# Feed-forward gate and up by seven block products instead of eight, down projection in six parts

## The chip, the cores and the metric

One core of a Trainium2 chip runs the kernel. The metric is the device time of one execution in microseconds (us), the median of the runs shown. The engines that matter here are PE (TensorE, matmuls), DVE (VectorE), ACT (ScalarE), POOL (GpSimd) and SP (SyncE, which issues the DMAs); each runs its own list of instructions in order, and semaphores make one wait for another.

## The reference

Two layers of a backbone over 512 latent tokens, with a context of 256 tokens that only the first layer updates. Each layer mixes tokens, projects back and then does a feed-forward step (`D_MODEL` 1024, `FFN_HIDDEN` 2816), all in float32:

```python
def swiglu(h, w_gate, w_up, w_down):
    return (jax.nn.silu(h @ w_gate) * (h @ w_up)) @ w_down
...
    for l in range(DEPTH):
        need_ctx = l < DEPTH - 1
        mx = (sc @ w_ada[l] + b_ada[l]).reshape(-1, N_MOD, 1, D_MODEL)
...
        h = modulate(rms_norm(x, g_ffn[l]), mx[:, 3], mx[:, 4])
        x = x + mx[:, 5] * swiglu(h, w_gate[l], w_up[l], w_down[l])
        if need_ctx:
            hc = modulate(rms_norm(ctx, g_ffn[l]), mc[:, 3], mc[:, 4])
            ctx = ctx + mc[:, 5] * swiglu(hc, w_gate[l], w_up[l], w_down[l])
```

## The kernel before

Tokens lie along the free axis, features on the 128 partitions: `xT` holds 8 blocks k of 128 features. Layer l=0 works on 768 tokens (512 latent and 256 context, `sts`), layer l=1 on the 512 latent ones. A float32 product is made of three fast products: each operand is split into a rounded high part and the rest (`h`, `l`), and high·high, low·high and high·low are summed in PSUM. So each 128x128 block of weights meets a stretch of tokens in three matmuls (`gemm`, L104).

A weight tile (`wtiles`, L205 to L217) is a DMA of 128x1024 into `wr`, a cast on ACT for the high part `wh` (L216), and a subtraction on POOL for the low part `wl` (L217). `wr`, `wh` and `wl` have two buffers each; `kh`, `kl` are the same for tiles that are kept.

The feed-forward step is the end of `layer()` (from L1302). The hidden 2816 features are 22 tiles t. For each t two weight tiles (gate, then up) are multiplied with all 8 blocks of `fh`, `fl` into two PSUM tiles `acc_gu` of two banks each (tag `b2`, four buffers), in stretches of 512 tokens and, in layer 0, 256 more. Then ACT takes the silu of the gate (L1340), DVE multiplies it by the up product (L1343, `av`), ACT rounds it (L1346, `ah`) and DVE subtracts (L1347, `al`). `FFN_PARTS` cuts the 22 tiles into three parts; at the end of a part the down projection multiplies the part's 7 or 8 tiles with 8 column blocks m of `w_dn` into `acc_d`, and DVE adds the result, scaled by `mod`, to `xT` (L1361). In the last part the column blocks in `KEPT` keep their weights and are done one stretch of tokens after the other.

```python
b2 = lambda nm: ps.tile([P, 1024], F32, tag="b2", name=nm, bufs=4)
...
for (t0, t1) in FFN_PARTS:
    for t in range(t0, t1):
        for j in range(2):
            gemm(acc, *w, hh, hl, sts if t else segs[1:])
            next(ada, None)
    for m in range(KD):
        gemm(acc, wh, wl, ah, al, sts)
        for st_ in sts:
            add(m, st_, acc[:, st_])
        next(ada, None)
```

`ada_rows` (L254) is a side task of layer 0's feed-forward step: 56 loads `wada` of 512 KB, each followed by two long DVE multiplications with a sum (`junk`), which give the modulation of what comes later. One step of it is taken at each `next(ada)`. Its first part, `mod[0][:, 5]`, scales the down projection of layer 0.

The norm ahead of the step (`norm_mod`, L297 to L305) makes `fh` and `fl` block by block from `xT`; it runs in two stretches of tokens, and the first two products start while it runs. The order of the instructions on each engine is set when the kernel is built, by a scheduler that takes the program's dependences, tile by tile; two products in one PSUM tile share its buffer, which is free again only when the last reader of either is done.

## Time and profile before

| what | value |
|---|---|
| median of 3 runs | 2154.72 us (2153.34 to 2160.51) |
| profiled execution | 2156.67 us, its span 2154.9 us |
| PE busy | 2003.9 us (93% of the span) |
| DVE, ACT, POOL busy | 1244.0, 707.8, 839.9 us |
| mean granted PE clock | 0.962 |
| layer 0's feed-forward step | about 684 to 1220 us of the span |
| layer 1's feed-forward step | about 1780 us to the end |

The span is the profiled time from the first to the last instruction; 1.8 us of the execution lie around it. A busy share says how much of the time an engine had an instruction in it. The granted clock is TensorE's: 1.00 is 2.4 GHz, 0.50 is 1.2 GHz.

### The profile page before, as it was taken

The page shows a single profiled execution, that of the slowest core. Times are in us where ns is not written, and L with a number is a line of the kernel's source. Part 1 is how long each engine was busy: PE and PEld are TensorE (multiplying, and loading weights), DVE is VectorE, ACT ScalarE, POOL GpSimd, SP SyncE. Part 2 cuts the span into 40 slices and gives each one's busy share as a digit, 9 for nine tenths or more (in the row PEclk, how much of TensorE's full clock was granted, in tenths as well). Part 3 has the DMA queues.
Part 4 walks back from the last instruction along what each step waited for, and adds up shares of the span by engine and source line. Part 5 has one row for each costly group of instructions (what it writes and reads, how often), then busy time and mean ns, then how long its engine had stood idle before and what let it go on. Part 6 is the DMA issues. An engine that isn't in the chain of part 4 may idle for free. (4 is left out here: it accounts for less than half of the span.)

```text
span 2154.9 us, 32133 instructions
## 1 busy us (share of the span) xinstructions
PE 2003.9 (93%) x12770; PEld 1694.8 (79%) x12770; DVE 1244.0 (58%) x2107; ACT 707.8 (33%) x1381; POOL 839.9 (39%) x602
## 2 busy tenths in 40 slices
...
GB/s 275 81 81 156 65 142 82 149 147 129 103 50 98 100 125 157 91 135 129 135 127 75 119 93 59 104 123 73 143 65 88 82 92 67 97 98 94 102 96 91
DMA packets 119278, 232.57 MB, mean 108 GB/s; under 512 B 30484, under 2 KB 55956, under 8 KB 119000
## 3 DMA queue, kind: packets, MB, share of 16 engines
...
## 5 line engine op out<-in xcount | busy, mean ns | idle before, releaser
L217 POOL TENSOR_TENSOR wl<-wr,wh 128x1024 fp32r<-128x1024 f32 (+2 forms) x188 | 440.0, 2341 | 716.4 <-ACT wh L216 708.0
L216 ACT CAST wh<-wr 128x1024 fp32r<-128x1024 f32 (+2 forms) x190 | 193.5, 1019 | 730.2 <-PE acc_gu L104 289.3
L104 PE MATMUL acc_gu<-fh,wh 128*128 128x512 f32 (+1 forms) x1024 | 359.2, 353 | 6.1 <-ACT fh L304 5.3
L104 PE MATMUL acc_gu<-fl,wh 128*128 128x512 f32 (+1 forms) x1024 | 361.0, 353 | 3.6 <-DVE fl L305 3.6
L104 PE MATMUL acc_gu<-fh,wl 128*128 128x512 f32 (+1 forms) x1024 | 360.2, 352 | 0.0
L104 PE MATMUL acc_in<-hh,wl 128*128 128x512 f32 (+1 forms) x640 | 227.3, 359 | 23.2 <-POOL wl L217 23.2
L104 PE MATMUL acc_in<-hh,wh 128*128 128x512 f32 (+1 forms) x640 | 229.9, 363 | 17.9 <-ACT xp L491 7.4
L104 PE MATMUL acc_in<-hl,wh 128*128 128x512 f32 (+1 forms) x640 | 229.8, 360 | 3.2 <-DVE hl L305 2.0
L1343 DVE TENSOR_TENSOR av<-acc_gu,av 128x768 f32<-128x768 f32 (+1 forms) x44 | 36.3, 825 | 337.5 <-PE acc_gu L104 330.0
L104 PEld LDWEIGHTS acc_gu<-fh,wh 128*128 128x128 f32 x1024 | 194.1, 190 | 33.2 <-ACT fh L304 6.9
L104 PEld LDWEIGHTS acc_gu<-fl,wh 128*128 128x128 f32 x1024 | 195.1, 191 | 29.8 <-DVE fl L305 3.9
L104 PEld LDWEIGHTS acc_gu<-fh,wl 128*128 128x128 f32 x1024 | 195.0, 190 | 26.5
L104 PEld LDWEIGHTS acc_in<-hh,wh 128*128 128x128 f32 x640 | 125.7, 197 | 43.4 <-ACT xp L491 9.1
L104 PEld LDWEIGHTS acc_in<-hh,wl 128*128 128x128 f32 x640 | 125.6, 198 | 43.0 <-POOL wl L217 25.4
L104 PE MATMUL acc_d<-al,wh 128*128 128x512 f32 (+1 forms) x444 | 157.2, 354 | 0.0
L104 PE MATMUL acc_d<-ah,wh 128*128 128x512 f32 (+1 forms) x444 | 157.2, 354 | 0.0
L104 PE MATMUL acc_d<-ah,wl 128*128 128x512 f32 (+1 forms) x444 | 156.1, 354 | 0.0
L254 DVE CUSTOM_DVE_ANT_0 junk<-wada,scb 128x1024 f32<-128x1024 f32 x112 | 145.6, 1300 | 6.3 <-DMA wada<-w_adaT 3.2
L104 PEld LDWEIGHTS acc_in<-hl,wh 128*128 128x128 f32 x640 | 126.5, 198 | 25.9 <-DVE hl L305 4.6
L501 DVE SCALAR_TENSOR_TENSOR cy<-xp,cw,cy 128x770 f32<-128x770 f32 (+1 forms) x96 | 128.2, 1335 | 22.2 <-ACT cy L499 18.4
L1361 DVE SCALAR_TENSOR_TENSOR xT<-acc_d,mod,xT 128x512 f32<-128x512 f32 (+1 forms) x76 | 46.5, 635 | 155.1 <-PE acc_d L104 155.1
L1347 DVE TENSOR_TENSOR al<-av,ah 128x768 fp32r<-128x768 f32 (+1 forms) x44 | 100.4, 2281 | 35.2 <-ACT ah L1346 35.2
...
## 6 DMA issues: line engine op xcount, KB each, us to landing
wr<-w_gu SPq DMA_DIRECT2D x88, 512.0 KB, 3.5
wada<-w_adaT SPq DMA_DIRECT2D x56, 512.0 KB, 3.4
wr<-w_in SPq DMA_DIRECT2D x48, 512.0 KB, 3.5
...
wada<-w_ada SPq DMA_DIRECT2D x24, 512.0 KB, 3.4
...
wr<-w_dn SPq DMA_DIRECT2D x16, 512.0 KB, 3.6
...
```

The lines of the kernel that those rows point to most:

```text
L104: nc.tensor.matmul(out, lhsT, rhs, start=start, stop=stop)
L216: S.copy(out=hi[:, sl], in_=raw[:, sl])
L217: eng.tensor_tensor(out=lo[:, sl], in0=raw[:, sl], in1=hi[:, sl].bitcast(F32), op=ALU.subtract)
L254: V.tensor_tensor_reduce(out=junk, in0=w, in1=scb[:, s], scale=1.0, scalar=0.0, op0=ALU.mult, op1=ALU.add, accum_out=mod[l][:, part, j, s: ...
L501: stt(out=y[:, :wid], in0=xp[:, j:j + wid], scalar=w_(j), in1=y[:, :wid], op0=ALU.mult, op1=ALU.add)
L1343: tt(out=av[:, :nT], in0=accs[1][:, :nT], in1=av[:, :nT], op=ALU.mult)
L1347: after.append(tt(out=l_[:, :nT], in0=av[:, :nT], in1=h_[:, :nT].bitcast(F32), op=ALU.subtract))
L1361: stt(out=xT[:, m, st_], in0=acc, scalar=mod[l][:, 5, m, s:s + 1], in1=xT[:, m, st_], op0=ALU.mult, op1=ALU.add)
```

## The change

For tiles t from 2 on, the two weight tiles of t and the activations are each cut into 2x2 blocks: the weights into gate and up (rows) by two halves of k, the activations into two halves of k by two halves of the tokens (`nh` = 384 in layer 0, 256 in layer 1). The eight block products become seven of sums of blocks (`seven`). Four activation sums t1 to t4 are made once per layer, four weight sums s1 to s4 for every t (`weights`), and seven additions from PSUM put the results together. Tiles 0 and 1 keep eight products (`first`), now done in two halves of the tokens. `split2` makes high and low parts; `FFN_ENG` says which engine does each weight sum and each low part (V is DVE, G is POOL). The down projection is done in six parts instead of three, with four buffers of `ah` and `al` instead of eight, and all 8 column blocks of the last part are kept. `ada_rows` has one `wada` buffer instead of two, and makes one column instead of two for four of layer 1's six parts. Lines of the changed kernel are numbered anew: `gemm` is L109, the weight sums L1402, the splits L1334 (ACT) and L1335, the additions from PSUM L1424, `junk` L264, the product of silu and up L1459, `ah` L1462, `al` L1463, the addition to `xT` L1479.

```diff
-FFN_PARTS = ((0, 8), (8, 15), (15, 22))
-
-KEPT = (4, 5, 6, 7)
+FFN_PARTS = ((0, 4), (4, 8), (8, 12), (12, 15), (15, 18), (18, 22))
+FFN_BUFS = 4
+
+FFN_ENG = (("VVVV", "GVGV"), ("VVVV", "GVVV"))
+
+ADA_T_ = (0, 3, 3, 3) + (0, 1) * 9
+
+KEPT = (0, 1, 2, 3, 4, 5, 6, 7)
...
+            ns = 2 if l == 0 or part < 2 else 1
-                w = sb.tile([P, D], F32, tag="wa", name="wada", bufs=2)
+                w = sb.tile([P, D], F32, tag="wa", name="wada", bufs=1)
                 nc.sync.dma_start(out=w, in_=a["w_adaT"][l, part, j])
                 with tc.issue_after(after[-1].ins):
-                    for s in range(2):
+                    for s in range(ns):
                         junk = sb.tile([P, D], F32, tag="junk", name="junk", bufs=1)
...
+        def split2(dst, src, eng):
+            S.copy(out=dst[0], in_=src)
+            eng.tensor_tensor(out=dst[1], in0=src, in1=dst[0].bitcast(F32), op=ALU.subtract)
+
+        def ffn_norm(k, cols, rs):
+            c, t = int(cols == CTX), xf[k][:, cols]
+            stt(out=t, in0=xT[:, k, cols], scalar=e.gs[l][:, 1, k, c:c + 1], in1=rs[:, :cols.stop - cols.start], op0=ALU.mult, op1=ALU.mult)
+            S.activation(out=t, in_=t, func=AF.Identity, bias=mod[l][:, 3, k, c:c + 1])
+            if k >= 4:
+                to = [(b2x[k - 4], cols, 0)]
+            else:
+                to = [(ts[k], slice(max(cols.start, h.start), min(cols.stop, h.stop)), h.start) for ts, h in ((b11, H[0]), (b12, H[1]))]
+            for hl_, c_, c0 in to:
+                if c_.start < c_.stop:
+                    split2([x[:, c_.start - c0:c_.stop - c0] for x in hl_], xf[k][:, c_], G if k % 2 else V)
+
...
+        fslot = lambda n: [fw.tile([P, 1024], F32R, tag="f" + x, name="f" + x, bufs=2)[:, 0:n] for x in "hl"]
+        wslot = lambda n: [e.wp.tile([P, 1024], F32R, tag="w" + x, name="w" + x, bufs=2)[:, 0:n] for x in "hl"]
...
+        at = lambda acc, h: acc[:, 512 * h:512 * h + nh]
+        blocks = (b11 + b21, b12 + b22)
+        first = [(whole(i // 2, i % 2, wslot if i < 2 else fslot), b2("acc_gu")) for i in range(3)]
+        for h, cols in enumerate(segs):
+            if h:
                 rs = e.rstd_of(xT, b2, sb, (cols,))[0]
             for k in range(KD):
-                e.norm_mod(xT, l, 1, sb, hh, hl, k, cols, rs)
-        second = [wtiles(a["w_gu"][l, 1, j], 1024, sg, 2) for j in range(2)]
+                ffn_norm(k, cols, rs)
+            for k in range(KD):
+                ws = slice(k * P, (k + 1) * P)
+                for w, acc in first:
+                    mm3(nc, at(acc, h), (w[0][:, ws], w[1][:, ws]), blocks[h][k], k == 0, k == KD - 1)
+        first.append((whole(1, 1, fslot), b2("acc_gu")))
+        for h in range(2):
+            prod(at(first[3][1], h), first[3][0], blocks[h])
+        for k in K4:
+            x11, x12, x21, x22 = xf[k][:, H[0]], xf[k][:, H[1]], xf[k + 4][:, H[0]], xf[k + 4][:, H[1]]
+            for i, (o, p_, q_, dst) in enumerate(((x11, x12, x11, t1_), (x12, x22, x12, t3_), (x22, x22, x11, t2_), (x21, x21, x22, t4_))):
+                tt(out=o, in0=p_, in1=q_, op=ALU.subtract)
+                split2(dst[k], o, G if i % 2 else V)
...
+            rg = e.wp.tile([P, 1024], F32, tag="wr", name="wr", bufs=2)
+            ru = fw.tile([P, 1024], F32, tag="fr", name="fr", bufs=1)
+            s_ = sb.tile([P, 1024], F32, tag="s", name="s", bufs=1)
+            for j, r_ in enumerate((rg, ru)):
+                nc.sync.dma_start(out=r_, in_=a["w_gu"][l, t, j])
+            lo_, hi_ = slice(0, 512), slice(512, 1024)
+            sum_ = lambda i, o, p_, q_, op=ALU.subtract: en[S_ENG[i]].tensor_tensor(out=o, in0=p_, in1=q_, op=op)
+            sum_(0, s_[:, lo_], ru[:, lo_], ru[:, hi_], ALU.add)
+            sum_(1, s_[:, hi_], s_[:, lo_], rg[:, lo_])
+            w1 = wslot(1024)
+            split2(w1, rg, en[L_ENG[0]])
+            w2 = fslot(1024)
+            split2(w2, s_, en[L_ENG[1]])
+            sum_(2, ru[:, lo_], rg[:, lo_], ru[:, lo_])
+            w3 = wslot(1024)
+            split2(w3, ru, en[L_ENG[2]])
+            sum_(3, rg[:, lo_], rg[:, hi_], s_[:, hi_])
+            w4 = fslot(512)
+            split2(w4, rg[:, lo_], en[L_ENG[3]])
+            f = lambda w, c: [x[:, c] for x in w]
+            return f(w1, lo_), f(w1, hi_), f(w2, lo_), f(w2, hi_), f(w3, lo_), w4, f(w3, hi_)
+
+        def seven(t, av, uw):
+
+            a11, a12, s1, s2, s3, s4, a22 = weights(t)
+            accs = [b2("acc_gu") for _ in range(4)]
+            m1_, m6_, m2_, m5_, m3_, m7_, m4_ = [at(accs[i // 2], i % 2) for i in range(7)]
+            g0, g1, u, w = av[:, H[0]], av[:, H[1]], uw[:, H[0]], uw[:, H[1]]
+            plus = lambda o, p_, q_: tt(out=o, in0=p_, in1=q_, op=ALU.add)
+            prod(m1_, a11, b11)
+            S.copy(out=g0, in_=m1_)
+            prod(m6_, s2, t2_)
+            plus(u, m6_, g0)
+            prod(m2_, a12, b21)
+            plus(g0, m2_, g0)
+            S.activation(out=g0, in_=g0, func=AF.Silu)
+            prod(m5_, s1, t1_)
+            plus(g1, m5_, u)
+            prod(m7_, s3, t3_)
+            plus(w, m7_, g1)
+            plus(u, m7_, u)
+            prod(m3_, s4, b22)
+            plus(g1, m3_, g1)
+            silu = S.activation(out=g1, in_=g1, func=AF.Silu)
+            prod(m4_, a22, t4_)
+            plus(u, m4_, u)
+            return silu
...
-                accs = []
-                for j in range(2):
-                    w, acc = (wtiles(a["w_gu"][l, t, j], 1024) if t > 1 else second[j], b2("acc_gu")) if t else first[j]
-                    gemm(acc, *w, hh, hl, sts if t else segs[1:])
...
+                    uw = sb.tile([P, nT], F32, tag="uw", name="uw", bufs=2)
+                    silu = seven(t, av, uw)
+                    if t == FFN_PARTS[-1][1] - 1:
+                        e.preload(silu)
+                    tt(out=av, in0=av, in1=uw, op=ALU.mult)
...
+                h_ = ap_.tile([P, nT], F32R, tag="ah", name="ah", bufs=FFN_BUFS)
+                l_ = ap_.tile([P, nT], F32R, tag="al", name="al", bufs=FFN_BUFS)
+                S.copy(out=h_, in_=av)
+                after.append(tt(out=l_, in0=av, in1=h_.bitcast(F32), op=ALU.subtract))
                 ah.append(h_)
                 al.append(l_)
+                for _ in range(ADA_T_[t] if l == 0 else 0):
+                    next(ada, None)
```

In the rows that follow, `out<-in` names the tiles with their buffer numbers, and `[waits X]` the engine or DMA queue that the instruction waits for. On PE, where one weight tile of layer 0 follows another in the kernel before (the buffer of tile 7300 was last used two t's of products earlier):

```order
L104 MATMUL acc_gu_7239<-fl7_6748,wh_7234 128x256
L104 MATMUL acc_gu_7239<-fh7_6740,wl_7235 128x256
L104 MATMUL acc_gu_7300<-fh0_6733,wh_7295 128x512 [waits DVE_49,Activation_49]
L104 MATMUL acc_gu_7300<-fl0_6741,wh_7295 128x512
L104 MATMUL acc_gu_7300<-fh0_6733,wl_7296 128x512 [waits Pool_49]
L104 MATMUL acc_gu_7300<-fh1_6734,wh_7295 128x512
```

In the changed kernel, layer 0, product m5 of one t (into the second half of PSUM tile 7992, with the token sum t1) is followed by product m2 of the next t (into tile 8128, which has the same buffer):

```order
L109 MATMUL acc_gu_7992<-t1h3_6756,fh_7977 128x384
L109 MATMUL acc_gu_7992<-t1l3_6757,fh_7977 128x384
L109 MATMUL acc_gu_7992<-t1h3_6756,fl_7978 128x384
L109 MATMUL acc_gu_8128<-gh0_6742,wh_8109 128x384 [waits DVE_49]
L109 MATMUL acc_gu_8128<-gl0_6743,wh_8109 128x384
L109 MATMUL acc_gu_8128<-gh0_6742,wl_8110 128x384
```

There the first matmul of m2 waits for DVE, whose addition of m5 (L1424) is the last reader of that buffer.

At the end of a part, before: PE in layer 0, second part. The down projection of the first column blocks (`acc_d_9298`, `acc_d_9355`) has begun with the tiles that are ready, and `ah_9288` is the part's last tile:

```order
L104 MATMUL acc_d_9298<-al_9160,wh_9293 128x512 [waits DVE_49]
L104 MATMUL acc_d_9298<-ah_9159,wl_9294 128x512
L104 MATMUL acc_d_9355<-ah_8512,wh_9350 128x512 [waits Activation_49]
L104 MATMUL acc_d_9355<-al_8513,wh_9350 128x512
L104 MATMUL acc_d_9298<-ah_9288,wh_9293 128x512 [waits Activation_49]
L104 MATMUL acc_d_9298<-al_9289,wh_9293 128x512 [waits DVE_49]
L104 MATMUL acc_d_9298<-ah_9288,wl_9294 128x512
```

Ahead of the row that waits for ACT stand 20 matmuls of the down projection (18 into `acc_d_9298`, two into `acc_d_9355`) behind the last product of the part.

At the end of a part, after: PE in layer 0, second part. `acc_gu_8259` holds product m3 of the part's last t, and `ah_8356`, `al_8357` are that t's activations:

```order
L109 MATMUL acc_gu_8259<-gh2_6746,fl_8254 128x384
L109 MATMUL acc_gu_8259<-gh3_6748,fh_8253 128x384
L109 MATMUL acc_gu_8259<-gl3_6749,fh_8253 128x384
L109 MATMUL acc_gu_8259<-gh3_6748,fl_8254 128x384
L109 MATMUL acc_d_8372<-ah_8356,wh_8367 128x512 [waits Activation_49]
L109 MATMUL acc_d_8411<-ah_8356,wh_8406 128x512
L109 MATMUL acc_d_8372<-al_8357,wh_8367 128x512 [waits DVE_49]
L109 MATMUL acc_d_8372<-ah_8356,wl_8368 128x512
```

Here the last product m3 stands directly ahead of the row that waits for its own activations; what the three ready tiles allowed (18 matmuls into `acc_d_8372` and `acc_d_8411`) stands ahead of m3, on both sides of m5.

On DVE, layer 0, after a down projection (`s`, `fr` and `wr` are weight sums, `fl` low parts, `uw` and `av` the additions from PSUM, `junk` the side task):

```order
L264 ISA junk_9496,mod1_89<-wada_9494,scb_7201 128x1024 [waits DMAHW3_49]
L264 ISA mod1_89 128x1
L1402 TENSOR_TENSOR s_9632<-fr_9631 128x512 [waits DMAHW5_49]
L1424 TENSOR_TENSOR uw_9499<-acc_gu_9525,av_9498 128x384 [waits PE_49,Activation_49]
L1402 TENSOR_TENSOR s_9632<-s_9632,wr_9630 128x512 [waits DMAHW1_49,DVE_49]
L1402 TENSOR_TENSOR fr_9631<-wr_9630,fr_9631 128x512 [waits Pool_49]
L1424 TENSOR_TENSOR av_9498<-acc_gu_9526,av_9498 128x384 [waits DVE_49]
L1402 TENSOR_TENSOR wr_9630<-wr_9630,s_9632 128x512 [waits DVE_49,Pool_49]
L1424 TENSOR_TENSOR av_9498<-acc_gu_9526,uw_9499 128x384 [waits PE_49]
L1424 TENSOR_TENSOR uw_9499<-acc_gu_9527,av_9498 128x384 [waits DVE_49]
L1424 TENSOR_TENSOR uw_9499<-acc_gu_9527,uw_9499 128x384
L1335 TENSOR_TENSOR fl_9642<-s_9632,fh_9641 128x1024 [waits Activation_49]
```

The additions into `av_9498` from `acc_gu_9526` (m2, then m5) stand behind a `junk` that waits for its DMA and behind weight sums of the next t; before, a t had two DVE instructions of its own (L1343 and L1347).

## Rows read from the trace of the kernel before

**Rows 1.** Windows in both steps: busy us, count by engine, clock, DMA share, GB/s.

```profile
700.00:1200.00 500.00, 500.00 (x2889) 442.91 (x2888) 241.61 (x327) 103.50 (x117) 140.64 (x60) 1.00 0.38 119
1800.00:2100.00 300.00, 300.00 (x1326) 248.47 (x1324) 75.69 (x58) 80.89 (x100) 131.43 (x57) 1.00 0.32 96
```

**Rows 2.** Timeline of PE, 512 wide: first and last of 37.

```profile
2111.78 0.39 PE L104 MATMUL acc_d<-al,wh 128*128 128x512 f32 x1
...
2119.94 0.39 PE L104 MATMUL acc_d<-al,wh 128*128 128x512 f32 x1
```

**Rows 3.** Timeline of PE, 256 wide: first and last of 22.

```profile
2138.29 0.28 PE L104 MATMUL acc_d<-ah,kl 128*128 128x256 f32 x1
...
2140.81 0.28 PE L104 MATMUL acc_d<-ah,kl 128*128 128x256 f32 x1
```

**Rows 4.** Lines by shape, 720 to 1220 us: busy us, mean ns, idle.

```profile
L254 DVE CUSTOM_DVE_ANT_0 junk<-wada,scb 128x1024 f32<-128x1024 f32 x110 | 143.1, 1301 | 6.3 <-DMA wada<-w_adaT 3.2 <-DVE xT L1361 0.3
L1347 DVE TENSOR_TENSOR al<-av,ah 128x768 fp32r<-128x768 f32 x21 | 46.9, 2232 | 19.0 <-ACT ah L1346 19.0
L1343 DVE TENSOR_TENSOR av<-acc_gu,av 128x768 f32<-128x768 f32 x21 | 20.1, 958 | 174.1 <-PE acc_gu L104 174.1
...
L217 POOL TENSOR_TENSOR wl<-wr,wh 128x1024 fp32r<-128x1024 f32 x47 | 113.0, 2404 | 282.5 <-ACT wh L216 282.5
...
L1346 ACT CAST ah<-av 128x768 fp32r<-128x768 f32 x21 | 17.6, 838 | 9.7 <-DVE av L1343 8.1
L1340 ACT ACTIVATE av<-acc_gu 128x768 f32<-128x768 f32 x20 | 16.1, 806 | 0.0
```

**Rows 5.** Lines by shape, layer 1, 1800 to 2100 us.

```profile
L1347 DVE TENSOR_TENSOR al<-av,ah 128x512 fp32r<-128x512 f32 x21 | 49.1, 2340 | 14.6 <-ACT ah L1346 14.6
L1343 DVE TENSOR_TENSOR av<-acc_gu,av 128x512 f32<-128x512 f32 x21 | 14.5, 692 | 148.8 <-PE acc_gu L104 148.8
...
L1346 ACT CAST ah<-av 128x512 fp32r<-128x512 f32 x21 | 13.0, 621 | 2.8 <-DVE av L1343 2.7
L1340 ACT ACTIVATE av<-acc_gu 128x512 f32<-128x512 f32 x22 | 12.9, 587 | 0.0
```

**Rows 6.** Tiles mxl and wl on DVE: minimum, median, maximum ns.

```profile
L1277 DVE TENSOR_TENSOR mxl<-dn_q,mxh x10: 672/684/689, 571.5 to 1710.4; 128x512 fp32r<-128x512 f32 x10
...
L217 DVE TENSOR_TENSOR wl<-wr,wh x2: 1226/1502/1778, 67.1 to 1521.8; 128x1024 fp32r<-128x1024 f32 x2
```

**Rows 7.** Timeline of DVE and POOL where they meet.

```profile
1850.05 2.44 DVE L1347 TENSOR_TENSOR al<-av,ah 128x512 fp32r<-128x512 f32 x1 [0.69 <-ACT ah L1346]
...
1849.54 2.39 POOL L217 TENSOR_TENSOR wl<-wr,wh 128x1024 fp32r<-128x1024 f32 x1 [3.05 <-ACT wh L216]
...
834.35 3.14 DVE L254 CUSTOM_DVE_ANT_0 junk<-wada,scb 128x1024 f32<-128x1024 f32 x1 [0.77 <-DMA wada<-w_adaT]
...
842.22 1.14 DVE L1361 SCALAR_TENSOR_TENSOR xT<-acc_d,mod,xT 128x512 f32<-128x512 f32 x2
...
834.01 2.40 POOL L217 TENSOR_TENSOR wl<-wr,wh 128x1024 fp32r<-128x1024 f32 x1 [6.40 <-ACT wh L216]
841.90 2.66 POOL L217 TENSOR_TENSOR wl<-wr,wh 128x1024 fp32r<-128x1024 f32 x1 [5.49 <-ACT wh L216]
```

**Rows 8.** Two pauses of PE, and windows from where they end.

```profile
684.09 1.22 PE L104 MATMUL acc_gu<-fh,wh 128*128 128x512 f32 x2 [3.18 <-ACT fh L304]
...
1476.39 0.50 PE L104 MATMUL acc_in<-hh,wl 128*128 128x512 f32 x1 [3.26 <-POOL wl L217]
...
684.00:693.00 9.00, 7.14 (x16) 5.17 (x17) 8.80 (x10) 3.48 (x7) 3.60 (x2) 0.50 0.66 188
1476.00:1484.00 8.00, 7.61 (x43) 6.72 (x44) 7.96 (x4) 1.22 (x2) 4.75 (x3) 1.00 0.57 120
```

**Rows 9.** DMA issues: KB each, median us from issue to landing.

```profile
wada<-w_adaT SPq DMA_DIRECT2D x56, 512.0 KB, 3.4
```

**Rows 10.** Timeline of DVE, start of layer 0's feed-forward norm.

```profile
681.34 4.05 DVE L297 SCALAR_TENSOR_TENSOR nt<-xT,gs,nrs 128x512 f32<-128x512 f32 x2
```

More of the change, by code (lines that the diff above doesn't have):

```diff
@@ L1285, in layer @@
     wb = [wtiles(a["w_out2"][l, i], 1024, mp, 2) for i in range(2)]
[L1286 to L1287 removed]
+    segs = sts if need_ctx else HALVES
     for st_ in segs:
```

72 lines of the change are left out of this document (42 added, 30 removed).

## Prediction

> **What bounds the kernel now.** I read the page first: PE is the only engine near full, and the windows show that in both feed-forward steps it is full. It is busy for 500.00 of 500 us in layer 0 and 300.00 of 300 in layer 1, at granted clock 1.00 [rows 1], with DVE at 242 us of the 500 and 76 us of the 300. So this stage is bound by the number of matmuls and their spacing, and every other engine has slack there: a removed matmul is worth its slot, and work added to DVE, ACT or POOL costs nothing until something on PE waits for it. The reader is to see in the timelines that a slot depends on the width: 36 slots of 512 columns take 2119.94 - 2111.78 = 8.16 us, 0.2267 us each [rows 2]; 21 slots of 256 take 2.52 us, 0.120 each [rows 3]. Nothing is 384 wide in the kernel before; halfway between the two is 0.1733 us, an estimate. A matmul lasts 0.39 or 0.28 us, so its result is there 0.16 us after its slot.
>
> **Products.** Before, a tile t of layer 0 takes 48 x (0.2267 + 0.120) = 16.64 us; with seven products it is 7 x 12 = 84 matmuls of 384, 14.56 us: 2.08 less, for 20 tiles 41.7 us. In layer 1, 48 x 0.2267 = 10.88 against 84 x 0.120 = 10.08: 0.80 less, 16.0 us for 20 tiles. The gain is smaller there because halving 512 to 256 costs 0.0067 us a slot. Tiles 0 and 1 keep 96 half-width matmuls: nothing in layer 0 (96 x 0.1733 = 16.64), 2 x (11.52 - 10.88) = 1.3 us lost in layer 1. Sum: **-56.4 us**, 2.6%. The down projection keeps its columns and widths; its 8 kept blocks in halves cost a fraction of a microsecond.
>
> The Trainium skill, "TensorE: Matmul & The Clock Gate", section "Back-to-back issue gap", gives an isolated slot as width/2.4 + 2.5 ns: 109, 162.5 and 216 ns here. By it the sum would be 20 x 1.95 + 20 x 1.21 - 0.2 = -63 us. The trace's slots are 5 to 10% longer [rows 2, 3], most for the narrow ones, so the rows decide.
>
> **The wait between m5 and m2.** The PSUM tile of m2 and m5 is one buffer, and the order has m2 of the next t directly behind m5 of this one. m2 must wait until DVE has read m5: 0.16 us to the result and one addition from PSUM. Such an addition takes 0.958 us at 768 columns [rows 4] and 0.692 at 512 [rows 5], so on that line 0.56 at 384 and 0.43 at 256. That is 0.72 us in layer 0 and 0.59 in layer 1 with DVE free; there are 14 such pairs within parts in each layer: **+18.4 us**. It can hardly be less; what more it is when DVE is not free is counted below.
>
> **The part boundaries.** Before, 20 matmuls (4.5 us) of the down projection lie between a part's last product and the first row that needs its last tile, and no idle time shows [rows 1]. Now m3 stands directly ahead of that row. From its last slot: 0.16; addition 0.56; silu of half the columns (0.806 at 768 and 0.587 at 512 [rows 4, 5], so 0.48 at 384); product with the up part 0.96; cast 0.838 [rows 4]; together 3.0 us. Then `al`, 0.95 us alone (0.684 at 512 [rows 6], by width near 1.0 at 768), less two matmuls: 0.5. So 3.5 us in layer 0. In layer 1: 0.16 + 0.43 + 0.37 + 0.69 + 0.621 [rows 5] = 2.27, and 0.23 for `al`: 2.5. Five boundaries in each layer have no cover (the sixth has the other tiles of all eight kept blocks): 17.5 + 12.5. The first one of layer 0 has a `junk` and its load ahead of the last `al`: the load takes 3.4 us [rows 9], with one buffer it starts after the `junk` before it, and I add 3. **+33 us**, bounds 27 and 38.
>
> **The clock.** Pauses of PE near 3 us can cost speed afterwards: after 3.18 us the granted clock was 0.50 for 9 us, after 3.26 us it stayed 1.00 [rows 8]. Layer 0's boundaries lie at that size. At half speed those 9 us lose up to 4.5; I take half of the five at 3 us: **+7 us**, bounds 0 and 20. Layer 1's pauses are shorter: nothing.
>
> **DVE beside POOL.** DVE's work per t rises from two instructions to about 16. Two-input operations in SBUF take 0.684 us at 512 and 1.226 at 1024 alone [rows 6]. Layer 0: four weight sums 2.7, splits 1.9, seven additions 3.9, product 0.96, `al` 1.0: 10.5 us of 15.3 that PE now needs (14.56 + 0.72). Layer 1: 2.7 + 3.1 + 3.0 + 0.69 + 0.68 = 10.2 of 10.7. But such an operation does not run beside POOL's: `al` of 512 takes 2.44 us when it meets a 2.39 us subtraction, against 0.684 alone, and a `junk` 3.14 [rows 7], 1.301 on average [rows 4]; with an operand in PSUM two additions took 1.14 us in all beside a POOL one [rows 7]. POOL has two subtractions of 2.4 us [rows 4] per t in layer 0 and one in layer 1. So layer 0 comes to 10.5 + 4.8 = 15.3, just PE's time, and with the two `junk` of every second t to 17.9: 2.6 too much for nine of them, of which I count half, 12 us, since DVE catches up in the down projections. Layer 1 comes to 10.2 and part of 2.4: about 11.1 against 10.7 for 14 tiles, 6 us. **+18 us**; bounds 0 (the holds fall on PSUM additions) and 45 (each t is held as `al` is).
>
> **The start.** The changed norm does eight scalings before the first low part, not two. Two took 4.05 us where POOL was busy [rows 10]; at 0.68 alone six more are 4 us in layer 0, at half the width 2 in layer 1: **+6 us**, bounds 0 and 12. Loads are as many bytes as before, and the 32 `junk` fewer save DVE time that PE never waited for [rows 1].
>
> **Sum.** -56.4 + 18.4 + 33 + 7 + 18 + 6 = +26.0. The profiled execution took 2156.67 us (span 2154.9 and 1.8 around it), 2 us over the median 2154.72. So 2182.7 - 2 = **2181 us**. About 0.3% (6.5 us) is what a measurement of this kernel tells from no change.
>
> **Rivals.**
> 1. Faster: DVE keeps ahead. Place: the additions from PSUM in front of m2, m5 and m7. If POOL's holds fall where DVE would wait for PE anyway, each t costs PE only the forced 0.72 and 0.59 us. Without the terms for DVE, clock and start, and with 30 us at the boundaries: -56.4 + 18.4 + 30 = -8, **2147 us**. It decides at 15.3 us of DVE time per t, holds counted, in layer 0 and 10.7 in layer 1. For it: DVE is idle half of the step now [rows 1], and 10.5 fits. Against: the `junk` pairs, and every `al` now meets a hold (mean 2.232 and 2.340 us [rows 4, 5]). 0.20.
> 2. Break-even: the holds half hidden, no drop of the clock: -8 + 3 + 9 = +4, 2159 us. 0.13.
> 3. The forecast, 2165 to 2200. 0.47.
> 4. DVE sets the pace in both layers. If at every t the two-input operations wait POOL out, layer 0 goes to 17.9 us per t with or without `junk` pairs, 2.6 over PE for 14 tiles, and layer 1 to 10.2 + 2.4 = 12.6, 1.9 over for 14: 63 us instead of 18, less the idle time that then covers boundaries and drops (some 15): +56, **2211 us**. 0.20. The Trainium skill, "SBUF — State Buffer", section "Who interferes with whom", states this as a rule: a VectorE instruction with two SBUF inputs contends with a GpSimd one that reads SBUF, and the loser is blocked for the whole instruction. The trace agrees (2.44 against 0.684 us [rows 6, 7]); the rule speaks against the change, but does not say how often they meet.
>
> The range 2140 to 2215 takes in the floor of rival 1 and rival 4; the forecast's own is 2165 to 2200. Faster 0.20, within 0.3% 0.13, slower 0.67.
>
> **What would show it.** In the changed profile: slots of 384 at 0.173 us and 256 at 0.120; per t within a part some 15.3 to 18 us in layer 0 and 11 in layer 1; pauses of PE of 0.6 to 0.8 us ahead of m2 ended by DVE's addition; ten pauses of 2.3 to 4 us ahead of a part's last `ah`, ended by ACT; `al` and weight sums at 2 us and more beside POOL. PE's share of the feed-forward steps would fall below 0.95. The forecast is wrong if the pauses ahead of m2 are absent, if the boundaries stay under 2 us, or if DVE waits for PE at every addition; on the other side, if 12.6 us per t appear in layer 1.

## The result, and the profile after

The changed kernel takes 2322.29 us (median of 4 runs, 2311.97 to 2337.5), against 2154.03 us of the kernel before on the same chip: a ratio of 1.0787, interval 1.076 to 1.0814. It is slower, as forecast, but by 168 us where the sum said 26; the range ended at 2215. The profiled execution took 2327.03 us, span 2325.2.

Where the time went shows in windows over the same four stretches of both kernels: from the first output projection to the first feed-forward product, and the feed-forward step, in each layer. Windows of the kernel before (columns as in [rows 1]: length, busy us and count of PE, weight loads, DVE, ACT, POOL, clock, DMA share, GB/s):

```profile
571.70:684.00 112.30, 105.92 (x656) 88.01 (x654) 68.11 (x140) 48.02 (x103) 37.54 (x22) 0.98 0.25 82
684.00:1242.50 558.50, 556.64 (x3175) 490.89 (x3176) 272.55 (x369) 123.45 (x149) 163.71 (x74) 0.99 0.39 122
1709.00:1772.10 63.10, 60.88 (x381) 50.88 (x379) 33.56 (x74) 27.32 (x59) 24.07 (x14) 1.00 0.37 116
1772.10:2144.00 371.90, 366.10 (x1723) 308.48 (x1724) 109.02 (x114) 113.70 (x164) 162.39 (x76) 0.99 0.30 90
```

Of the changed kernel:

```profile
571.40:705.30 133.90, 112.48 (x657) 91.68 (x655) 67.83 (x142) 49.53 (x106) 40.17 (x23) 0.92 0.24 77
705.30:1339.90 634.60, 559.30 (x2935) 516.36 (x2936) 445.61 (x628) 188.08 (x289) 207.12 (x115) 0.94 0.33 106
1801.50:1885.40 83.90, 70.19 (x411) 58.03 (x409) 38.77 (x83) 32.76 (x71) 29.84 (x18) 0.92 0.35 108
1885.40:2314.40 429.00, 378.10 (x2504) 342.34 (x2504) 283.28 (x437) 168.15 (x294) 131.09 (x93) 0.96 0.26 75
```

The reader is to see two things. First, the lengths: +21.6, +76.1, +20.8 and +57.1 us, 175.6 together (the rest of the program is 5 us shorter). A quarter of the loss lies ahead of the steps that the change is about. Second, PE: before it was busy for 556.64 of 558.50 us; now it has 240 matmuls fewer in layer 0's step, is busy just as long, and stands idle for 75.3 us besides.

Counting each step's matmuls by width at the full-clock slots separates these. In layer 0 the work falls from 550.6 to 509 us, in layer 1 from 361.7 to 346.6: by this count, matmuls times slots, the seven products are worth 57 us, as forecast. Against that stand idle time, from 1.9 to 75.3 and from 5.8 to 50.9 us, and slots that are longer than at full clock, from 6 to 50 and from 4.3 to 31.5 us. More than half of the latter is the clock: a mean of 0.94 over 634.6 us is some 76 us at half clock, which lose at most 38; 0.96 over 429 us loses at most 17 (at most, since idle time at half clock loses nothing). Before, 0.99 over both steps loses 9. So of 71 us more in longer slots the clock explains some 46; what makes the other 25 isn't shown.

The slot of 384 columns is what halfway between the neighbours gave. From the first to the last of 17 records in PE's timeline of layer 0's step, 16 slots take 2.78 us, 0.174 each:

```profile
961.25 0.34 PE L109 MATMUL acc_gu<-t3l,wh 128*128 128x384 f32 x1
...
964.03 0.33 PE L109 MATMUL acc_gu<-t4l,wh 128*128 128x384 f32 x1
```

What PE waited for, from the waits of the changed kernel, first in layer 0's step (705 to 1340 us; columns: us in total, times, longest):

```profile
PE acc_gu L109 <- DVE av L1424: 19.7, 11, 4.1
PE acc_d L109 <- ACT ah L1462: 16.0, 5, 3.8
...
PE acc_gu L109 <- POOL wl L1335: 7.5, 5, 2.5
PE acc_gu L109 <- DVE uw L1424: 4.8, 5, 1.8
...
PE acc_d L109 <- DVE al L1463: 2.6, 5, 1.6
```

and in layer 1's (1885 to 2315 us):

```profile
PE acc_d L109 <- ACT ah L1462: 14.8, 6, 3.1
PE acc_gu L109 <- DVE av L1424: 12.0, 15, 1.4
PE acc_gu L109 <- DVE uw L1424: 6.0, 4, 2.7
```

The two waits that the forecast named are there and lead both lists: PE behind the addition of m5 or m2 (L1424), and PE at the part boundaries (`ah`, and behind it `al`). In layer 0 five boundaries cost 16.0 + 2.6 us, in layer 1 six cost 14.8.

One wait shows why the first kind is longer than 0.72 us. PE, DVE and POOL of the changed kernel, around 850 us (PE's timeline, then DVE's, then POOL's):

```profile
849.58 0.34 PE L109 MATMUL acc_gu<-fh,wl 128*128 128x384 f32 x1
854.00 0.45 PE L109 MATMUL acc_gu<-gh,wh 128*128 128x384 f32 x1 [4.08 <-DVE av L1424]
...
849.50 2.83 DVE L1402 TENSOR_TENSOR wr<-wr,s 128x512 f32<-128x512 f32 x1
852.25 1.21 DVE L264 CUSTOM_DVE_ANT_0 junk<-wada,scb 128x1024 f32<-128x1024 f32 x1
853.40 0.55 DVE L1424 TENSOR_TENSOR av<-acc_gu,uw 128x384 f32<-128x384 f32 x1
...
849.07 2.71 POOL L1335 TENSOR_TENSOR wl<-fr,wh 128x1024 fp32r<-128x1024 f32 x1 [6.55 <-PE acc_gu L109]
```

PE's product ends at 849.92. The addition that PE's next product needs takes 0.55 us, but DVE starts it only at 853.40: a weight sum that meets POOL's subtraction takes 2.83 us, not 0.684 [rows 6], and a `junk` of 1.21 us comes next in DVE's order. The next product starts at 854.00.

And pauses of this size cost clock. PE's timeline of the changed kernel at a part boundary, and ahead of another m2:

```profile
790.95 0.34 PE L109 MATMUL acc_gu<-gh,fl 128*128 128x384 f32 x1
795.05 1.22 PE L109 MATMUL acc_d<-ah,wh 128*128 128x512 f32 x2 [3.76 <-ACT ah L1462]
797.85 0.80 PE L109 MATMUL acc_d<-al,wh 128*128 128x512 f32 x1 [1.57 <-DVE al L1463]
...
891.46 0.44 PE L109 MATMUL acc_gu<-gh,wh 128*128 128x384 f32 x1 [2.17 <-DVE av L1424]
```

Windows of it that begin where those pauses, and the one at 850 us, have ended:

```profile
797.90:803.90 6.00, 6.00 (x24) 5.61 (x25) 2.48 (x3) 0.62 (x1) 1.27 (x1) 0.50 0.27 87
854.00:858.00 4.00, 4.00 (x15) 4.00 (x16) 3.61 (x5) 0.97 (x1) 0.00 (x0) 0.64 0.75 262
891.50:896.00 4.50, 4.50 (x17) 4.50 (x18) 3.16 (x5) 0.62 (x1) 0.86 (x1) 0.63 0.48 147
```

Behind pauses of 3.76 and 1.57, of 4.08, and of 2.17 us PE is full, and yet at 0.50, 0.64 and 0.63 of its clock: at 1.2 GHz for all or most of each window. It isn't so behind every pause: of the 25 of 2 us and more in the two steps 21 are followed by half clock, while behind two of 2.12 us in layer 0 and two of 2.34 us in layer 1 it stayed at 1.00.

### The profile page after: what moved, and what is told of

Same layout as the page of the kernel before. It is cut to its first block, busy times and chain, and to the rows that moved or that the text cites. A ratio compares the mean times of both kernels' runs of the same rounds, so it can differ in the third digit from the quotient of the medians.

```text
span 2325.2 us, 34515 instructions
## 1 busy us (share of the span) xinstructions
PE 2037.1 (88%) x13310; PEld 1768.8 (76%) x13310; DVE 1591.2 (68%) x2693; ACT 829.0 (36%) x1657; POOL 852.0 (37%) x664
## 3 DMA queue, kind: packets, MB, share of 16 engines
q1 hardware_dynamic: 126040, 230.52, 31.7%
## 5 line engine op out<-in xcount | busy, mean ns | idle before, releaser
L226 POOL TENSOR_TENSOR wl<-wr,wh 128x1024 fp32r<-128x1024 f32 (+3 forms) x144 | 249.5, 1735 | 515.1 <-ACT wh L225 457.5
L109 PE MATMUL acc_in<-hh,wl 128*128 128x512 f32 (+1 forms) x640 | 228.4, 360 | 21.5 <-POOL wl L226 21.5
L109 PE MATMUL acc_in<-hh,wh 128*128 128x512 f32 (+1 forms) x640 | 231.2, 365 | 12.7 <-ACT xp L502 3.7
L109 PE MATMUL acc_in<-hl,wh 128*128 128x512 f32 (+1 forms) x640 | 230.1, 360 | 1.4 <-POOL hl L313 1.1
L225 ACT CAST wh<-wr 128x1024 fp32r<-128x1024 f32 (+3 forms) x146 | 111.7, 767 | 324.6 <-PE acc_d L109 105.6
L1335 POOL TENSOR_TENSOR wl<-wr,wh 128x1024 fp32r<-128x1024 f32 x44 | 111.6, 2535 | 208.4 <-ACT wh L1334 208.4
L109 PE MATMUL acc_d<-ah,wh 128*128 128x512 f32 (+1 forms) x432 | 159.4, 373 | 30.5 <-ACT ah L1462 27.7
L264 DVE CUSTOM_DVE_ANT_0 junk<-wada,scb 128x1024 f32<-128x1024 f32 x80 | 118.0, 1475 | 77.1 <-DMA wada<-w_adaT 76.6
L109 PE MATMUL acc_d<-al,wh 128*128 128x512 f32 (+1 forms) x432 | 161.2, 373 | 2.6 <-DVE al L1463 2.6
L109 PEld LDWEIGHTS acc_in<-hh,wl 128*128 128x128 f32 x640 | 126.5, 199 | 41.8 <-POOL wl L226 23.9
L109 PE MATMUL acc_d<-ah,wl 128*128 128x512 f32 (+1 forms) x432 | 158.0, 368 | 0.2
L109 PEld LDWEIGHTS acc_in<-hh,wh 128*128 128x128 f32 x640 | 126.7, 199 | 38.7 <-issue 6.9
L109 PEld LDWEIGHTS acc_in<-hl,wh 128*128 128x128 f32 x640 | 126.9, 198 | 22.1 <-POOL hl L313 2.2
L1479 DVE SCALAR_TENSOR_TENSOR xT<-acc_d,mod,xT 128x512 f32<-128x512 f32 (+1 forms) x152 | 92.0, 632 | 68.2 <-PE acc_d L109 67.9
L109 PEld LDWEIGHTS acc_d<-ah,wh 128*128 128x128 f32 x432 | 85.1, 199 | 50.2 <-ACT ah L1462 30.3
L688 POOL TENSOR_TENSOR tmp<-R,Bk 96x1 f32<-96x1 f32 (+30 forms) x62 | 77.8, 1255 | 93.6 <-DVE R L689 83.7
L109 PEld LDWEIGHTS acc_d<-al,wh 128*128 128x128 f32 x432 | 87.0, 201 | 17.9 <-DVE al L1463 7.2
L109 PEld LDWEIGHTS acc_d<-ah,wl 128*128 128x128 f32 x432 | 86.3, 200 | 12.8 <-POOL wl L226 1.5
L1335 POOL TENSOR_TENSOR wl<-fr,wh 128x1024 fp32r<-128x1024 f32 x20 | 54.6, 2731 | 95.9 <-ACT wh L1334 73.0
L688 DVE TENSOR_TENSOR tmp<-R,Bk 96x1 f32<-96x1 f32 (+30 forms) x62 | 85.2, 1374 | 6.0 <-DMA Bk<-d_blk 5.0
L109 PE MATMUL acc_gu<-gh,wh 128*128 128x384 f32 (+1 forms) x192 | 65.3, 340 | 25.0 <-DVE av L1424 24.2
```

Source lines behind the costliest of these rows:

```text
L109: nc.tensor.matmul(out, lhsT, rhs, start=start, stop=stop)
L225: S.copy(out=hi[:, sl], in_=raw[:, sl])
L226: eng.tensor_tensor(out=lo[:, sl], in0=raw[:, sl], in1=hi[:, sl].bitcast(F32), op=ALU.subtract)
L264: V.tensor_tensor_reduce(out=junk, in0=w, in1=scb[:, s], scale=1.0, scalar=0.0, op0=ALU.mult, op1=ALU.add, accum_out=mod[l][:, part, j, s: ...
L688: (V if d == 0 else G).tensor_tensor(out=t_, in0=R[:, d, js, js], in1=bc1(Bk[:, js, i], s), op=ALU.mult)
L1335: eng.tensor_tensor(out=dst[1], in0=src, in1=dst[0].bitcast(F32), op=ALU.subtract)
```

## The experiments

The theory after the result: PE loses time in four places, and longer slots behind its pauses add to each. They are the moved memory ahead of the steps, the shared buffer of m5 and m2, DVE's order (held beside POOL, and filled by the side task), and the part boundaries. The rivals: the six parts or the move of pools alone explain nearly all, or DVE is simply overloaded. Ratios are against the kernel before; differences from the changed kernel are of the medians.

### Two parts of the change on their own, and m5 in a tile of its own

To the kernel before, only the six parts:

```diff
-FFN_PARTS = ((0, 8), (8, 15), (15, 22))
+FFN_PARTS = ((0, 4), (4, 8), (8, 12), (12, 15), (15, 18), (18, 22))
-KEPT = (4, 5, 6, 7)
+KEPT = (0, 1, 2, 3, 4, 5, 6, 7)
-                h_ = ap_.tile([P, T], F32R, tag="ah", name="ah", bufs=8)
-                l_ = ap_.tile([P, T], F32R, tag="al", name="al", bufs=8)
+                h_ = ap_.tile([P, T], F32R, tag="ah", name="ah", bufs=4)
+                l_ = ap_.tile([P, T], F32R, tag="al", name="al", bufs=4)
```

> The kernel before, with eight products, but its down projection in six parts, four buffers of ah and al, and all eight blocks of the last part kept. If the pauses at the boundaries (34 us in the changed profile) come from the order in which the seven products leave m3 last, plain products can put 18 matmuls of the three ready tiles behind the last product (4.1 us against a chain of 2.8): 2155 to 2170 us. If six parts cost this by themselves, and the clock with it: 2190 to 2220 us.

Measured: 2176.04 us, ratio 1.0105 (1.0082 to 1.0128), 22 us. This lies between the two expectations. (Four tiles are only eight steps of the side task, so the first column block of the first down projection is scaled without its bias.) Windows of both steps:

```profile
681.50:1240.80 559.30, 556.32 (x3176) 489.44 (x3176) 293.31 (x416) 131.16 (x175) 180.26 (x99) 0.99 0.37 121
...
1774.50:2163.60 389.10, 375.92 (x1735) 308.14 (x1736) 117.33 (x140) 114.93 (x183) 164.51 (x100) 0.98 0.29 87
```

Layer 0's step stays at 559; layer 1's is 389.1 against 371.9. So with eight products, the boundaries have their cover in layer 0, and the cost of three more down projections per layer is nearly all in layer 1, where I had given it no term. PE doesn't wait for `ah` or `al` in either step of this kernel; its largest wait in layer 1 that isn't of the norm is for the casts of weight tiles (`wh`, 3.8 us in three).

To the kernel before, only the order of the pools (`sb_fn` is opened ahead of `mixd`, and `es_a` is closed earlier, as the change needs for its larger tiles):

```diff
+    es_r = ExitStack()
+    sb = pool(es_r, f"sb_fn{l}", 2, side=A_)
     mp = pool(es_a, f"mixd{l}", side=A_)
...
-    segs, es_r = sts if need_ctx else HALVES, ExitStack()
-    sb = pool(es_r, f"sb_fn{l}", 2, side=A_)
+    segs = sts if need_ctx else HALVES
...
+    es_a.close()
     es_m.close()
...
-        es_a.close()
```

> The kernel before, with only the memory for the feed-forward norm opened ahead of that of the output projection, and the latter closed earlier, as the change does. In the changed profile the stretch from the first output projection to the first feed-forward product is 21 us longer in layer 0 and 21 us in layer 1. If the placement of the memory makes these: +25 to +40 us. If the new norm with its split tiles makes them: within 6 us of the kernel before.

Measured: 2189.69 us, ratio 1.0178 (1.0154 to 1.0202): 36 us from an edit that leaves every computation as it was. The two stretches ahead of the steps:

```profile
565.60:696.30 130.70, 112.52 (x657) 91.72 (x655) 64.70 (x140) 48.18 (x103) 38.79 (x23) 0.93 0.25 82
1724.90:1803.70 78.80, 68.34 (x410) 56.45 (x409) 36.24 (x82) 29.15 (x64) 23.76 (x14) 0.95 0.29 95
```

They are 18.4 and 15.7 us longer than before, which is nearly all of the 36. The tile `mxl`, operand of the output projection, first in this kernel and then in the changed one:

```profile
L1279 DVE TENSOR_TENSOR mxl<-dn_q,mxh x10: 677/682/692, 618.0 to 1752.5; 128x512 fp32r<-128x512 f32 x10
```

```profile
L1290 DVE TENSOR_TENSOR mxl<-dn_q,mxh x10: 680/683/693, 623.9 to 1829.7; 128x512 fp32r<-128x512 f32 x10
```

Its first instance stood at 571.5 us [rows 6]; now it comes at 618.0 and 623.9, behind a wait for PE's `o_mla`, a product of the stage before (2.4 and 3.0 us), which it doesn't wait for in the kernel before. By the order of the pools `mixd`, moved down in memory, shares its place with tiles of that stage and waits for their last readers; the trace shows the wait, not the addresses. The output projection, which had filled PE's pauses in that stage, now follows it: in layer 0's stretch PE is idle for 18.2 us, before for 6.4.

To the changed kernel, m5 in the free half of m4's PSUM tile, which takes away the wait between m5 and the next m2:

```diff
-            m1_, m6_, m2_, m5_, m3_, m7_, m4_ = [at(accs[i // 2], i % 2) for i in range(7)]
+            m1_, m6_, m2_, m5_, m3_, m7_, m4_ = [at(accs[i // 2], i % 2) for i in (0, 1, 2, 7, 4, 5, 6)]
```

> The changed kernel, with m5 put into the free half of m4's PSUM tile instead of m2's, so that m2 of the next t does not wait for the addition of m5. If each wait of PE costs its own time and the clock after it: 25 to 45 us less than the changed kernel, 2275 to 2300 us. If DVE sets the pace, the wait turns up at the next product: 2310 to 2325 us.

Measured: 2291.14 us, ratio 1.0648 (1.0624 to 1.0671), 31 us less. Its steps:

```profile
701.60:1323.70 622.10, 555.73 (x2936) 519.40 (x2937) 432.94 (x628) 190.13 (x289) 207.17 (x115) 0.93 0.32 108
1866.10:2276.00 409.90, 374.33 (x2504) 342.07 (x2504) 278.72 (x437) 169.79 (x294) 129.86 (x93) 0.96 0.25 79
```

12.5 us come back in layer 0 and 19.1 in layer 1. Of the idle time of the two steps 24 us go (126.2 to 102.0), and the rest comes back as shorter slots. 102 us of idle time stay. PE's waits for `av` are all but gone, 31.7 to 0.6 us, but those for `uw`, the addition of another product, rise from 10.8 to 35.4 us. The two lines for `uw`, layer 0's first:

```profile
PE acc_gu L109 <- DVE uw L1424: 21.8, 7, 4.7
PE acc_gu L109 <- DVE uw L1424: 13.6, 5, 2.9
```

Those for the low parts `fl` rise too, from 2.0 to 12.9 us. So the time is that of the first expectation, while much of the wait turned up at the next product, as the second has it: the shared buffer is one cause among several, and what stands in DVE's order stays in PE's way.

### The side task, POOL, and a later down projection

The side task cut to 8 of 1024 columns, loads and `junk` alike, so that the modulation rows lack most of their sums (a kernel without the side task gave no time):

```diff
-                w = sb.tile([P, D], F32, tag="wa", name="wada", bufs=1)
-                nc.sync.dma_start(out=w, in_=a["w_adaT"][l, part, j])
+                w = sb.tile([P, 8], F32, tag="wa", name="wada", bufs=1)
+                nc.sync.dma_start(out=w, in_=a["w_adaT"][l, part, j][:, 0:8])
```

> The changed kernel with the side task of layer 0's feed-forward step cut to 8 of 1024 columns: its loads and its 80 long DVE instructions become tiny, and the modulation rows it makes are left short of the rest of their sums. If these instructions, behind their loads and behind POOL, make DVE late in layer 0: 30 to 60 us less than the changed kernel, 2262 to 2292 us, all of it in layer 0's feed-forward step. If POOL's holds of the weight sums and splits make DVE late: less than 12 us, over 2310 us.

Measured: 2275.09 us, ratio 1.0568 (1.0542 to 1.0594), 47 us less, nearly all in layer 0:

```profile
702.40:1290.70 588.30, 544.54 (x2935) 503.38 (x2936) 348.19 (x628) 188.47 (x289) 194.37 (x115) 0.96 0.21 65
```

DVE is busy 97 us less, and PE's step 46 us shorter (634.6 to 588.3). PE's waits for `av` there fall from 19.7 to 3.5 us. The edit takes loads away with the DVE time (65 GB/s against 106). DVE's line for `junk` (720 to 1290 us) tells the two apart in part:

```profile
L264 DVE CUSTOM_DVE_ANT_0 junk<-wada,scb 128x8 f32<-128x8 f32 x80 | 25.7, 322 | 62.8 <-DMA wada<-w_adaT 62.0
```

In the changed kernel `junk` was busy for 118.0 us, and DVE stood idle for 76.6 us for its loads; before, for 3.2 [rows 4]. Most of that waiting stays here, so what went is above all the time of `junk` itself. Two buffers of `wada` instead of one, as before, were not tried.

All low parts of the feed-forward steps on DVE, none on POOL:

```diff
-FFN_ENG = (("VVVV", "GVGV"), ("VVVV", "GVVV"))
+FFN_ENG = (("VVVV", "VVVV"), ("VVVV", "VVVV"))
```

> The changed kernel with the splits of gate and up that POOL did (two of 1024 columns per t in layer 0, one in layer 1) on DVE, so that no subtraction of POOL meets DVE there: DVE gets 2.4 us more of its own work per t in layer 0 and 1.2 in layer 1, and loses the holds. In the changed profile the holds come to about 2.8 us per t in layer 0 (the sum over its groups of mean less the time alone). If holds are only one part of why DVE is late: 2310 to 2345 us. If the holds are what sets the pace: 2270 to 2300 us.

Measured: 2269.3 us, ratio 1.0555 (1.053 to 1.0581), 53 us less, though DVE now does 60 subtractions more. Groups of DVE's instructions by line and shape in layer 0's step (busy us, mean ns, idle before them), of the changed kernel:

```profile
L264 DVE CUSTOM_DVE_ANT_0 junk<-wada,scb 128x1024 f32<-128x1024 f32 x80 | 118.0, 1475 | 77.1 <-DMA wada<-w_adaT 76.6
L1335 DVE TENSOR_TENSOR fl<-s,fh 128x1024 fp32r<-128x1024 f32 x20 | 34.1, 1707 | 0.7 <-ACT fh L1334 0.7
...
L1402 DVE TENSOR_TENSOR s<-fr 128x512 f32<-128x512 f32 x20 | 24.4, 1222 | 21.4 <-DMA fr<-w_gu 17.6 <-POOL t4l L1335 3.8
L1463 DVE TENSOR_TENSOR al<-av,ah 128x768 fp32r<-128x768 f32 x21 | 22.0, 1048 | 5.4 <-ACT ah L1462 5.4
```

and of this one:

```profile
L264 DVE CUSTOM_DVE_ANT_0 junk<-wada,scb 128x1024 f32<-128x1024 f32 x80 | 104.8, 1310 | 51.6 <-DMA wada<-w_adaT 51.1
L1335 DVE TENSOR_TENSOR fl<-s,fh 128x1024 fp32r<-128x1024 f32 x20 | 24.5, 1223 | 0.0
...
L1402 DVE TENSOR_TENSOR s<-fr 128x512 f32<-128x512 f32 x20 | 13.7, 686 | 9.2 <-DMA fr<-w_gu 5.4 <-POOL t4l L1335 3.8
```

Its window of the step:

```profile
700.30:1301.40 601.10, 546.70 (x2936) 507.51 (x2937) 438.44 (x668) 189.68 (x289) 101.02 (x75) 0.95 0.34 112
```

The means fall to those of an operation alone (1223 and 686 ns; 1.226 and 0.684 us in [rows 6]). DVE takes over 40 instructions in this step and is busy 7 us less: what it gains from not being held pays for the work. DVE's load hardly changes, so an overload of DVE can't be what the 53 us were. Nor is it that PE gets these low parts sooner: its waits for them, 7.5 and 3.5 us on POOL in the two layers, become 6.5 and 1.3 on DVE. Its waits for `av` fall from 31.7 to 16.0 us.

In layer 1, the down projection of a part emitted behind the next part's first t, with five buffers of `ah` and `al`:

```diff
-FFN_BUFS = 4
+FFN_BUFS = (4, 5)
...
+                if t == t0 and late:
+                    down(*late)
+                    late = None
+            late = t0, t1, ah, al
+            if l == 0 and t1 < 22:
+                down(*late)
+                late = None
```

> The changed kernel, with layer 1's down projection of a part written after the first t of the next part (five buffers of ah and al there), so that PE has products of that t while the last activations of a part are made. Layer 1 has six pauses ended by ah, 14.8 us in all. If these cost their time and the clock after it: 15 to 30 us less than the changed kernel, 2292 to 2307 us, in layer 1 alone. If the pause only moves to another wait of PE on DVE: within 8 us of it.

Measured: 2311.17 us, ratio 1.0757 (1.0732 to 1.0782). Layer 1's step is 24 us shorter in the profile, 405.0 us against 429.0, while the median falls by only 11, with runs that spread over 13 us here and 26 in the changed kernel. PE's wait for `ah` in it falls from 14.8 us in six to 1.9 in one, and those for `av` stay at 12.1 us. So the boundaries' pauses are what they were taken for.

The three together (m5 apart, small side task, late down projection in both layers), again without most of the side task's sums:

> The changed kernel with three of the edits together: m5 apart from m2, the side task cut to 8 columns, and the late down projection in both layers. What stays is the products (-57 us against the kernel before), the moved memory (+36 by itself) and DVE's own load. If the pauses and the clock after them make the rest of the loss, most of it goes: 2160 to 2200 us. If DVE's load by itself sets the pace: over 2230 us.

Measured: 2234.62 us, ratio 1.0388 (1.0364 to 1.0412). By its number this is the second expectation, but DVE is busy for only 349 of the 570 us from 704 to 1274. In layer 0's step one wait now leads:

```profile
PE acc_gu L109 <- DVE uw L1424: 18.3, 6, 3.8
```

The pauses have gone from `ah` to an addition (L1424) of the t that now stands there. DVE's timeline ahead of the longest one, 3.80 us to 844.89:

```profile
841.47 0.69 DVE L1402 TENSOR_TENSOR s<-fr 128x512 f32<-128x512 f32 x1 [4.71 <-DMA fr<-w_gu]
...
844.19 0.55 DVE L1424 TENSOR_TENSOR uw<-acc_gu,av 128x384 f32<-128x384 f32 x1
```

No hold and no `junk` here: DVE is idle for 4.71 us, since the weight sums of the next t stand ahead of the addition in its order and the first of them waits for its load.

### Together

The three and all low parts on DVE, with the small side task as above:

> The three edits together (m5 apart, side task cut to 8 columns, late down projection in both layers), and all splits of gate and up on DVE. The three left 64 us of pauses and 44 us of lower clock in the two feed-forward steps, the pauses ended by the additions of m6 and by splits. If POOL's holds are still in these: 25 to 45 us less than the three edits, 2190 to 2210 us. If the holds reached PE only through what the three edits removed: within 10 us of 2235 us.

Measured: 2195.87 us, ratio 1.0203 (1.0167 to 1.024). Its two steps:

```profile
702.10:1249.20 547.10, 526.08 (x2935) 497.33 (x2936) 364.15 (x670) 189.09 (x288) 92.31 (x73) 0.98 0.22 68
1817.40:2191.70 374.30, 358.04 (x2504) 334.08 (x2504) 278.61 (x457) 168.62 (x294) 85.96 (x73) 0.99 0.28 87
```

547.1 + 374.3 = 921.4 us, 9 us less than the 930.4 of the kernel before. With these four causes out of the way the steps are faster than with eight products, by a sixth of the 57 us that the matmuls are worth; 21 and 16 us of idle time are left. Ahead of the steps this kernel loses 21.7 and 25.1 us, much as the changed one does, and 13.5 more in layer 1's mixing between them (480.0 us against 466.5, at a clock of 0.89 against 0.93); why that is, no run shows.

What leaves nothing out (m5 apart, all low parts on DVE, late down projection in layer 1):

> The changed kernel with the edits that leave nothing out: m5 apart, all splits of gate and up on DVE, late down projection in layer 1. Alone they gave 31, 53 and 11 us. If they act on different pauses: 2220 to 2235 us. If DVE is then late for want of time (13 us of own work per t in layer 0 with the products at 15): 2245 to 2265 us.

Measured: 2226.72 us, ratio 1.0351 (1.0309 to 1.0392), 95.6 us less than the changed kernel, where the three alone gave 31 + 53 + 11 = 95: they add up, within the spread of these runs (14 us here, 26 in the changed kernel).

The opposite way for layer 1, all four low parts on POOL:

```diff
-FFN_ENG = (("VVVV", "GVGV"), ("VVVV", "GVVV"))
+FFN_ENG = (("VVVV", "GVGV"), ("VVVV", "GGGG"))
```

> The changed kernel with all four splits of layer 1 on POOL instead of one: DVE loses 3.1 us of its own work per t and POOL gets 6, so that POOL is busy for some 8.5 of 10.7 us, and the weight sums, the product and al on DVE meet it each time. If the holds, not DVE's own load, make PE wait: 15 to 50 us more than the changed kernel, 2337 to 2372 us, all in layer 1. If DVE's own load does: 10 to 25 us less.

Measured: 2321.4 us, ratio 1.0801 (1.0764 to 1.0838): no change, and a miss for both expectations. Layer 1's step:

```profile
1876.90:2307.80 430.90, 380.50 (x2503) 344.00 (x2504) 251.45 (x377) 167.47 (x294) 265.19 (x153) 0.96 0.24 75
```

DVE has 60 instructions fewer and is busy only 32 us less, since those that stay are held: `al` takes 1372 ns on average and the third weight sum 1337. PE's time is the same. So it isn't DVE's load that PE's time follows, nor the number of subtractions on POOL alone; which operations are held, and what waits behind them, these runs don't separate further.

The pools of layer 1 opened where they were, in the changed kernel and in the whole one:

```diff
     es_r = ExitStack()
-    sb = pool(es_r, f"sb_fn{l}", 2, side=A_)
+    if l == 0:
+        sb = pool(es_r, f"sb_fn{l}", 2, side=A_)
     mp = pool(es_a, f"mixd{l}", side=A_)
...
-    mxl = mp.tile([P, 4, T], F32R, name="mxl")
+    mxl = mp.tile([P, 4, nT], F32R, name="mxl")
...
+    if l == 1:
+        sb = pool(es_r, f"sb_fn{l}", 2, side=A_)
...
-    es_a.close()
+    if l == 0:
+        es_a.close()
...
```

> The changed kernel, with the memory of layer 1's feed-forward norm opened again behind that of the output projection, as before (the projection's tiles are cut to the 512 tokens used, to make room). In the kernel before, the moved memory alone cost 16 us in layer 1. If that holds in the changed kernel too: 12 to 20 us less than it, 2302 to 2310 us, between layer 1's first output projection and its first feed-forward product. If the stretch is longer there because of the new norm: within 5 us of it.

> The kernel with m5 apart, all splits on DVE and the late down projection in layer 1 (2226.7 us), with layer 1's memory put back as in the run beside it. Layer 1's feed-forward step took 376 us there against 372 before. If the parts add up: 2207 to 2215 us, so still slower than the kernel before, by layer 0 and by layer 0's moved memory. If pauses ahead of the step only move into it: over 2220 us.

Measured: 2313.42 us, ratio 1.0754 (1.0717 to 1.0791), and 2213.52 us, ratio 1.0274 (1.0253 to 1.0295). The first is 9 us less than the changed kernel, between its two expectations; the second is as expected. Layer 1 of the latter:

```profile
1746.00:1818.40 72.40, 66.31 (x410) 53.78 (x408) 40.43 (x88) 34.18 (x76) 29.31 (x17) 0.97 0.39 125
1818.40:2190.10 371.70, 358.63 (x2504) 336.23 (x2504) 275.88 (x452) 166.54 (x290) 89.70 (x73) 0.98 0.28 87
```

The stretch ahead of the step takes 74.4 us in the first (83.9 in the changed kernel) and 72.4 here; the kernel before needs 63.1. So the move of memory is worth some 10 us there. Some 10 more come from elsewhere; the longer norm may be among them, which no run shows. The step, 371.7 us, is level with 371.9 before. In layer 0 undoing the move wasn't tried. No version made here beats the kernel before.

## Why the prediction was right or wrong

- **Products** (-56.4 us): right. The slots are 0.174 and 0.120 us, and the work of the two steps fell by 57 us.
- **The wait between m5 and m2** (+18.4): right in kind, too small in size. It was priced with DVE free at once; the waits for `av` come to 31.7 us of idle time. That taking the shared buffer away gave 31 us is no measure of that: the waits for `av` went, but 35 us of others came at `uw` and `fl`, and the part boundaries' fell.
- **The part boundaries** (+33): right in the two layers together, 16.0 + 2.6 and 14.8 us. But three more parts by themselves make layer 1's step 17 us longer, which had no term.
- **DVE beside POOL** (+18): the mechanism was right and the way of counting wrong; this is the first of the three steps that failed. I added up DVE's time per t against PE's, so that a hold counted only where the sum passed 15.3 us. DVE is busy for 446 of 635 us in layer 0's step. But it works in order, and PE waits for single additions: a weight sum held to 2.83 us and a `junk` behind it put 4.08 us on PE at 850 us, however idle DVE is later, and a load that DVE waits for did the same in the kernel with three edits. Without POOL's low parts the time falls by 53 us, with the small side task by 47. With one buffer of `wada` I added 3 us for a single boundary, and DVE waited 76.6 us for those loads. My row for the holds was also the wrong one: `al`, 2.232 us on average before [rows 4], now takes 1.05; the weight sums and splits are held instead. The Trainium skill, "SBUF — State Buffer", section "Who interferes with whom", calls the ports that VectorE and GpSimd share an exclusive lock; the trace agrees, 2.83 us beside a POOL subtraction of 2.71. Rival 4 fails like the forecast, since it let DVE's load set the pace; its 17.9 us per t without a `junk` pair doesn't follow either, as 10.5 and 4.8 are 15.3.
- **The clock** (+7): the second failed step. I let only layer 0's five boundaries drop it, half of the times. The slots lost 50 + 31 us, where 6 + 4 were lost before, and the clock is some 46 of the 71 more. Of 25 pauses of 2 us and more 21 were followed by half clock here, in both layers and at DVE's additions too. "Half of the times" came from two pauses that I had set side by side; in that same trace, of the kernel before, 17 of 19 pauses of 2 us and more were followed by half clock, and the one of 3.26 us was an exception. Over the steps of the changed kernel and nine of the others the lost slots are 0.6 to 0.9 us for each us of idle time, mostly near 0.7: 50 for 75, 17 for 21 and 31 for 46 in layer 0 of the changed kernel, the four together, and the whole one. On that average 3 us of idle time cost about 5, an estimate that takes in the longer slots that the clock doesn't explain.
- **The start** (+6): the third. I priced six more scalings and called the early closing of a pool nothing at all. The two stretches ahead of the steps grew by 42 us, and moving the pools alone costs the kernel before 36.

So the direction was right for reasons that were partly right, and the size was wrong: 26 us in the sum, 168 measured. Without the three terms that failed the sum is -5, so the direction hung on them too. Against their terms the clock in the steps is some 39 us over (46 for 7), the start 36, and the idle time within the steps 50 (119 for 18.4 + 33 + 18), in large part DVE's order; 25 us of slots that are longer for another reason had no term. These 150 are the gap of 142, but for 5 us that the rest of the program saves and rounding.
